# Four chunks and three parts of a product: part by part in place of chunk by chunk, with the weights at another place in their tiles

## The chip, the cores and the metric

The kernel runs on one core of a Trainium2 chip. Its engines each follow their own list of instructions and wait for each other through semaphores: TensorE (PE; its weight loads are shown apart as PEld), VectorE (DVE), ScalarE (ACT), GpSimd (POOL) and SyncE (SP), which issues most DMAs. The metric is the time of the device in microseconds for one whole execution, the median of several runs.

## The reference

One inference step of one decoder layer over 576 tokens: 512 of one new sequence and 8 x 8 of sampled sequences that have a retention state. Everything is float32.

```python
def swiglu(h, w_gate, w_up, w_down):
    return (jax.nn.silu(h @ w_gate) * (h @ w_up)) @ w_down
...
    h = modulate(rms_norm(x, n1_g), sh1, sc1)
    x = x + 0.5 * g1 * swiglu(h, w1_gate, w1_up, w1_down)
    h = modulate(rms_norm(x, nm_g), sh2, sc2)
    mix, S_new, v_rows = token_mix(h, pos0, S0, w_in, gm_ln_g, gm_ln_b, gm_ws, gm_bs, w_a, w_b, w_o)
    x = x + g2 * mix
    h = modulate(rms_norm(x, n2_g), sh3, sc3)
    x = x + 0.5 * g3 * swiglu(h, w2_gate, w2_up, w2_down)
```

The width is 1024, the inner width of each SwiGLU 2816. `token_mix` multiplies h by `w_in` (1024 x 10240), runs the gated spatial mixing and the retention over its columns, and goes back through `w_a`, `w_b` and `w_o`.

## The kernel before, in words

**Operands in two parts.** A float32 number is written as the sum of a high part, rounded to the format that a fast matmul takes (`F32R`), and a low part, the rest. ACT writes the high part by a copy; DVE then writes the low part, the source less the high part. A product of two such numbers takes three matmuls, high by high, high by low and low by high; low by low is dropped. In the code `wh, wl` are the parts of the weights, the left operand that is loaded into TensorE, and `xh, xl` those of the activations, the right operand that streams past.

**Pairs.** The gate and up columns of the two SwiGLUs, and most of `w_in`, go two columns of 128 at a time through seven block products of a Strassen-Winograd scheme in place of eight (class `Pair`; the first two pairs of each stage go plainly with eight, class `Plain`). The contraction of 1024 is split into two halves of 512, and the tokens into two halves of 288. So one block product, `prod` (line 647), is 512 x 128 by 512 x 288: four chunks of 128 of the contraction times three parts, twelve matmuls of 128 x 128 by 128 x 288 into one accumulator. There are 482 of them.

**Where the operands lie.** The right operands of `prod` are tiles `xa` and `xs` of 2 parts x 4 chunks x 288 elements: a chunk is 1152 bytes, the low part lies 4608 bytes behind the high one. They are made once for a stage, in two halves of two chunks (names such as `N11h0`, `N11h1`, `N11l0`, `N11l1` in the lists of steps: operand, part, half). The left operands are tiles `whl` (two column blocks) and, for `a12` alone, `whs` (one): 2 parts x blocks x 512 elements, with some elements of room. `put_hi` (line 664) takes a tile and lets ACT write the high part; `put_lo` lets DVE write the low part. `set_in` leaves the room partly ahead of the weights: they begin `at` elements into the tile. Every such tile begins at a multiple of 128 bytes. `whl` without an argument begins at `INTO`, 28 elements, which is 112 bytes. Other weights take `MID`, 45 elements or 180 bytes: those of the down projections (`wd`, `xw`, some `whl`) and of the mixing stage. One tile of `w_o`, `wo`, begins at 16 elements, 64 bytes. These go through `proj` (line 485), which has the same three matmuls for each chunk, with 320 or 256 tokens.

**What sets the order.** In the stages around a norm an order written out by hand (`BEGIN`, `INTO_MIX`, `INTO_FFN2`) says which step follows which, and each engine but SP is held to it. Elsewhere the calls of the code are placed by the scheduler of the programming layer, which at a few places puts matmuls of one product between those of another. A matmul waits for the last of its operands' writers, by a semaphore on the first matmul that needs it.

Of the kernel before, what the change touches and what calls it, by code (L numbers as in the profile page):

```python
# [15 lines left out]
P = 128  # L16
# [20 lines left out]

INTO = 28
MID = 45
HALF = (slice(0, H), slice(H, T))  # L40
PART = (slice(0, 320), slice(320, T))
PW = (320, T - 320)
# [42 lines left out]
def layer_kernel(ctx: ExitStack, tc: tile.TileContext, a):  # L85
# [7 lines left out]
    wp = ctx.enter_context(tc.tile_pool(name="wp", bufs=1))  # L93
# [16 lines left out]
    def nm(s):  # L110
        count[0] += 1
        return f"{s}_{count[0]}"


    now = {"wraw": None, "slu": None}
# [21 lines left out]
    def nine_w(shape):  # L137

        room = 9 * 256 - shape[1] * shape[2] * shape[3]
        return set_in(now["xs1"], shape, room, MID, tag="x", name=nm("xw"), bufs=3)  # L140

# [6 lines left out]
    def set_in(home, shape, room=INTO, at=INTO, **kw):  # L148

        n = 1  # L150
        for d in shape[1:]:
            n *= d
        t = home.tile([P, n + room], F32R, **kw)[:, at:at + n]
        if len(shape) == 4:
            return t.rearrange("p (a b c) -> p a b c", b=shape[2], c=shape[3])
        return t.rearrange("p (a b c d) -> p a b c d", b=shape[2], c=shape[3], d=shape[4])
# [9 lines left out]
    def whl(shape, at=INTO):  # L166
        small = len(shape) == 3 and shape[1] == 1
        tag = "whs" if small else "whl"
        return set_in(
            now["whs"] if small else wp, [P] + shape, INTO if small else 64, at,  # L170
            tag=tag, name=nm(tag), bufs=1 if small else 4,
        )

# [7 lines left out]
    def high_low(shape, at=INTO):  # L181
        t = whl([2] + shape, at)
        return t[:, 0], t[:, 1]
# [7 lines left out]
    def load_w(src, k0, kc, c0, cols, eng=None, at=INTO):  # L191
        return split_w(load_raw(src, k0, kc, c0, cols), eng, at)
# [39 lines left out]
    def tick(us):  # L232
        for s in list(side):
            s[1] -= us
            while s in side and s[1] <= 0:
                try:
                    s[1] += next(s[0])
                except StopIteration:
                    side.remove(s)
# [176 lines left out]
    class Norm:  # L416
# [4 lines left out]
        def square(self, x, h):  # L421
            if self.all is None:
                self.all = tp.tile([P, T], F32, tag="all", name=nm("all"), bufs=1)
                self.acc = [self.all[:, HALF[i]] for i in range(2)]
            first = self.n[h] == 0 and not self.t[h]
            t = self.acc[h] if first else half()
            self.t[h].append(t)
            ACT.activation(out=t, in_=x[:, HALF[h]], func=AF.Square)

# [65 lines left out]
    def cost(kc):  # L495
        return kc * 3 * 0.1225
# [26 lines left out]
    class Operands:  # L523
# [27 lines left out]
        def blocks(self, j):  # L551
            hb = self.hb
            return tuple(hb[:, c:c + 2, cl] for c in (2 * j, 4 + 2 * j) for cl in HALF)

# [56 lines left out]
    def norm_steps(st, n, O, h):  # L611
# [4 lines left out]
        for p in range(4):  # L616
            st[f"x{p}{h}"] = lambda p=p: O.x(p, n.r[h], HALF[h])
            for c in range(2):
                if h:
                    st[f"b{p}{c}"] = lambda p=p, c=c: O.b(2 * p + c, slice(H, NP))  # L620
                else:
                    st[f"b{p}{c}0"] = lambda p=p, c=c: O.b(2 * p + c, HALF[0])

# [22 lines left out]

    def prod(ps, w, x, fresh):
        (wh, wl), (xh, xl) = w, x
        for j in range(4):
            for z, (s, m) in enumerate(((wh, xh), (wh, xl), (wl, xh))):  # L650
                PE.matmul(  # L651
                    ps[:, :H], lhsT=s[:, j * P:(j + 1) * P], rhs=m[:, j, :],
                    start=fresh and j == 0 and z == 0, stop=j == 3 and z == 2, skip_group_check=True,
                )
        tick(cost(4))
# [6 lines left out]

    class Weights:
        def put_hi(self, names, src, neg=False):
            hl = whl([2, len(names), 512])
            if neg:
                ACT.activation(out=hl[:, 0], in_=src, func=AF.Copy, scale=-1.0)
            else:
                ACT.copy(out=hl[:, 0], in_=src)  # L669
            self.hl[names] = hl, src, neg  # L670
# [29 lines left out]
    class Plain(Weights):  # L700
# [22 lines left out]
        def h0a(self):  # L723
            self.A = [bank() for _ in range(2)]
            for ps, w in zip(self.A, ("n11", "n21")):
                prod(ps, self.w[w], op("N11"), True)
# [4 lines left out]
        def h1a(self):  # L731
            self.D = [bank() for _ in range(2)]
            for ps, w in zip(self.D, ("n11", "n21")):
                prod(ps, self.w[w], op("N1"), True)

        def h0b(self):
            for ps, w in zip(self.A, ("a12", "a22")):
                prod(ps, self.w[w], op("B21"), False)
# [5 lines left out]
        def e0s(self):  # L744
            self.g = self.g or self.gated()
            ACT.activation(out=self.g[:, HALF[0]], in_=self.A[0][:, :H], func=AF.Silu)

# [217 lines left out]
    def home_wd(c, shape):  # L965
        return set_in(now["hl"], shape, 64, MID, tag="wd", name=nm("wd"), bufs=2)

    def home_whl(c, shape):
        return home_wd(c, shape) if c in (0, 1, 4, 5) else whl(shape[1:], MID)

# [62 lines left out]
    for i in range(2):  # L1033
        for n in range(NT):
            m = P if n < 4 else NS
# [98 lines left out]
    def home1(c, shape):  # L1134
        if c in (6, 7):
            return nine_w(shape)
        return home_wd(c, shape) if c in (0, 1, 4, 5) else whl(shape[1:], MID)

# [400 lines left out]
    def weights_b(hds, j):  # L1539
        kc = 2 * len(hds)  # L1540
        return load_w(a["w_b"][0], 2 * hds[0], kc, j * (8 // kc) * P, 8 // kc * P, at=MID)

# [112 lines left out]
    def weights_u(g):  # L1655
        return load_w(win, 0, KC, U0 + g * P, P, at=MID)

# [78 lines left out]
    for i in range(2):  # L1736
        for n in range(NT):
            m, z = P if n < 4 else NS, NT * i + n
# [316 lines left out]
```

## Time and profile before

| | |
|---|---|
| median of 3 runs | 1657.79 us (1654.53 to 1658.67) |
| the profiled execution's own time | 1656.22 us |
| its span, first to last instruction | 1654.4 us |
| mean clock granted to TensorE | 0.996 |
| busy: PE, PEld, DVE, ACT, POOL | 1624.5, 1560.9, 1153.0, 784.3, 293.1 us |
| matmuls, weight loads | 12548, 12548 |
| of these in `prod`, line 651 | 5784 |
| moved by DMA | 252.09 MB, mean 152 GB/s |

A row of the profile names a line of the kernel (L651 is the matmul in `prod`, L485 that in `proj`, L669 and L679 the copies and subtractions of `put_hi` and `put_lo`, L564 and L571 those of the operands), an engine, an operation, and `out<-in` by the names of the tiles. Matmuls overlap: one of 288 columns takes some 294 ns from its start to its end, and the next begins long before that. How fast TensorE goes is read from the distance between starts, and in the rows in order of time from the start of one group to that of the next, divided by the count.

### The profile page before, as it was taken

The page shows a single profiled execution, that of the slowest core. Times are in us where ns is not written, and L with a number is a line of the kernel's source. Part 1 is how long each engine was busy: PE and PEld are TensorE (multiplying, and loading weights), DVE is VectorE, ACT ScalarE, POOL GpSimd, SP SyncE. Part 2 cuts the span into 40 slices and gives each one's busy share as a digit, 9 for nine tenths or more (in the row PEclk, how much of TensorE's full clock was granted, in tenths as well). Part 3 has the DMA queues.
Part 4 walks back from the last instruction along what each step waited for, and adds up shares of the span by engine and source line. Part 5 has one row for each costly group of instructions (what it writes and reads, how often), then busy time and mean ns, then how long its engine had stood idle before and what let it go on. Part 6 is the DMA issues. An engine that isn't in the chain of part 4 may idle for free. (4 is left out here: it accounts for less than half of the span.)

```text
span 1654.4 us, 31368 instructions
## 1 busy us (share of the span) xinstructions
PE 1624.5 (98%) x12548; PEld 1560.9 (94%) x12548; DVE 1153.0 (70%) x1835; ACT 784.3 (47%) x1331; POOL 293.1 (18%) x372
## 2 busy tenths in 40 slices
PE   8999999999999999999999999999999999999997
PEld 4899999999999999999999999998999999999997
DVE  6867857676697777854788554676848868676773
ACT  5634524344564556553444454453236525343454
POOL 0000000000411111113346343454231000000002
PEclk9999999999999999999999999999999999999999
DMA  9553444332536776765367575799540233332331
GB/s 301 145 156 109 141 133 136 114 103 87 179 117 209 227 213 189 222 192 192 121 192 251 180 171 159 207 262 271 172 141 14 87 93 96 95 92 81 99 89 58
DMA packets 300213, 252.09 MB, mean 152 GB/s; under 512 B 13594, under 2 KB 260634, under 8 KB 300067
## 3 DMA queue, kind: packets, MB, share of 16 engines
q1 hardware_dynamic: 284594, 206.76, 41.5%
q0 software_dynamic: 13168, 40.97, 8.9%
q10 hardware_dynamic: 2304, 2.36, 0.4%
q8 instruction: 98, 1.61, 0.4%
q14 instruction: 49, 0.39, 0.1%
HBM read 207.01 MB, written 43.02 MB: 151 GB/s over the span
## 5 line engine op out<-in xcount | busy, mean ns | idle before, releaser
L651 PE MATMUL ps<-xa,whl 128*128 128x288 f32 x3000 | 423.6, 296 | 5.8 <-ACT xa L564 2.4
L651 PEld LDWEIGHTS ps<-xa,whl 128*128 128x128 f32 x3000 | 404.5, 190 | 18.5 <-issue 4.2
L651 PE MATMUL ps<-xs,whl 128*128 128x288 f32 x2040 | 289.1, 295 | 0.9 <-ACT sn L660 0.5
L651 PEld LDWEIGHTS ps<-xs,whl 128*128 128x128 f32 x2040 | 274.0, 189 | 11.0 <-issue 4.2
L679 DVE TENSOR_TENSOR whl<-wraw,whl 128x1024 fp32r<-128x1024 f32 x192 | 234.4, 1223 | 55.0 <-ACT whl L669 46.7
L669 ACT CAST whl<-wraw 128x1024 fp32r<-128x1024 f32 x192 | 200.0, 1047 | 107.9 <-DVE wraw L793 65.9
L485 PEld LDWEIGHTS ps<-c,wd 128*128 128x128 f32 x1824 | 236.9, 188 | 3.5 <-issue 3.4
L485 PE MATMUL ps<-c,wd 128*128 128x320 f32 (+1 forms) x1824 | 240.0, 292 | 0.0
L485 PE MATMUL ps<-c,whl 128*128 128x256 f32 (+1 forms) x1368 | 186.9, 294 | 1.1 <-ACT c L195 0.7
L485 PEld LDWEIGHTS ps<-c,whl 128*128 128x128 f32 x1368 | 179.4, 188 | 3.4 <-ACT c L195 1.1
L472 POOL TENSOR_TENSOR x<-x,s 128x64 f32<-128x64 f32 x72 | 36.8, 511 | 797.4 <-DVE s L471 771.6
L466 DVE SCALAR_TENSOR_TENSOR x<-ps,gate,x 128x320 f32<-128x320 f32 (+1 forms) x128 | 61.1, 481 | 111.2 <-PE ps L485 111.1
L660 ACT COPY sn<-ps 128x288 f32<-128x288 f32 x195 | 77.4, 399 | 107.2 <-PE ps L651 106.9
L188 DVE TENSOR_TENSOR whl<-wraw,whl 128x1024 fp32r<-128x1024 f32 x56 | 76.3, 1364 | 66.2 <-ACT whl L187 65.4
L952 ACT CAST wd<-wraw 128x640 fp32r<-128x640 f32 (+2 forms) x58 | 45.4, 783 | 102.3 <-PE ps L485 93.4
L1353 PE MATMUL ps<-whl,xx 128*128 128x256 f32 x768 | 88.9, 276 | 0.0
L1353 PEld LDWEIGHTS ps<-whl,xx 128*128 128x128 f32 x768 | 88.0, 188 | 0.0
L651 PE MATMUL ps<-xs,whs 128*128 128x288 f32 x480 | 69.9, 294 | 0.0
L187 ACT CAST whl<-wraw 128x1024 fp32r<-128x1024 f32 x56 | 58.6, 1049 | 21.5 <-PE ps L485 13.3
L651 PEld LDWEIGHTS ps<-xs,whs 128*128 128x128 f32 x480 | 65.7, 189 | 0.0
L669 ACT CAST whs<-wraw 128x512 fp32r<-128x512 f32 x62 | 38.5, 620 | 56.5 <-PE ps L651 46.7
L957 DVE TENSOR_TENSOR wd<-wraw,wd 128x640 fp32r<-128x640 f32 (+2 forms) x58 | 53.5, 922 | 10.3 <-ACT wd L952 10.2
(285 smaller groups left out, 2220.6 us busy)
## 6 DMA issues: line engine op xcount, KB each, us to landing
ada<-in_w_ada_dram SPq DMA_DIRECT2D x56, 512.0 KB
wraw<-in_w_in_dram SPq DMA_DIRECT2D x96, 256.0 KB
wraw<-in_w_gate_dram SPq DMA_DIRECT2D x88, 256.0 KB
wraw<-in_w_up_dram SPq DMA_DIRECT2D x88, 256.0 KB
wraw<-in_w_in_dram SPq DMA_DIRECT2D x32, 512.0 KB
wraw<-in_w_down_dram SPq DMA_DIRECT2D x32, 384.0 KB
wraw<-in_w_down_dram SPq DMA_DIRECT2D x32, 320.0 KB
accd<-c POOLq DMA_DIRECT2D x32, 288.0 KB, 5.7
```

Source lines behind the costliest of these rows:

```text
L187: ACT.copy(out=hi, in_=raw)
L188: now["lo"] = (eng or DVE).tensor_tensor(out=lo, in0=raw, in1=hi.bitcast(F32), op=ALU.subtract)
L466: DVE.scalar_tensor_tensor(out=x[:, o:o + w], in0=ps[:, :w], scalar=g[:, c, 0:1], in1=x[:, o:o + w], op0=ALU.mult, op1=ALU.add)
L472: return lambda: POOL.tensor_tensor(out=x[:, NP:T], in0=x[:, NP:T], in1=u, op=ALU.add)
L485: PE.matmul(ps[:, :PW[h]], lhsT=s[:, k, c0:c0 + P], rhs=m[:, PART[h]], start=k == 0 and z == 0, stop=k == kc - 1 and z == 2,)
L651: PE.matmul(ps[:, :H], lhsT=s[:, j * P:(j + 1) * P], rhs=m[:, j, :], start=fresh and j == 0 and z == 0, stop=j == 3 and z == 2, skip_group ...
L660: ACT.copy(out=t, in_=ps[:, :H])
L669: ACT.copy(out=hl[:, 0], in_=src)
L679: now["lo"] = DVE.tensor_tensor(out=hl[:, 1], in0=src, in1=hl[:, 0].bitcast(F32), op=ALU.subtract)
L952: ACT.copy(out=hl[:, 0], in_=self.raw[c])
L957: DVE.tensor_tensor(out=lo, in0=self.raw[c], in1=hi.bitcast(F32), op=ALU.subtract)
L1353: PE.matmul(ps[:, :DV], lhsT=s, rhs=m, start=i == 0, stop=i == 23)
```

## The change

Three edits. `prod` has its loops swapped: the three parts are now the outer loop and the four chunks the inner one. The first part is high weights by the low operand, then high by high, then low weights by the high operand; before, high by high came first. And the weights that `put_hi` places begin 7 elements, 28 bytes, into their tile in place of 112; the small tiles have 64 elements of room in place of 28, and their weights begin at 39 elements, 156 bytes, which is again 28 past a multiple of 128. Other weights stay where they are, and so does the number of instructions.

```diff
@@ -37,6 +37,7 @@
 
 INTO = 28
 MID = 45
+EARLY = 7
 HALF = (slice(0, H), slice(H, T))
@@ -167,7 +168,7 @@
         small = len(shape) == 3 and shape[1] == 1
         tag = "whs" if small else "whl"
         return set_in(
-            now["whs"] if small else wp, [P] + shape, INTO if small else 64, at,
+            now["whs"] if small else wp, [P] + shape, 64, at + 32 if small else at,
             tag=tag, name=nm(tag), bufs=1 if small else 4,
         )
 
@@ -646,8 +647,8 @@
 
     def prod(ps, w, x, fresh):
         (wh, wl), (xh, xl) = w, x
-        for j in range(4):
-            for z, (s, m) in enumerate(((wh, xh), (wh, xl), (wl, xh))):
+        for z, (s, m) in enumerate(((wh, xl), (wh, xh), (wl, xh))):
+            for j in range(4):
                 PE.matmul(
                     ps[:, :H], lhsT=s[:, j * P:(j + 1) * P], rhs=m[:, j, :],
                     start=fresh and j == 0 and z == 0, stop=j == 3 and z == 2, skip_group_check=True,
@@ -662,7 +663,7 @@
 
     class Weights:
         def put_hi(self, names, src, neg=False):
-            hl = whl([2, len(names), 512])
+            hl = whl([2, len(names), 512], EARLY)
```

The order of the instructions is shown at three places. The first is on TensorE in the second SwiGLU's gate and up columns (1292.8 to 1294.5 us in the profile): a product with fresh weights `whl_14896`, whose high part comes from ACT and whose low part from DVE, and with it a second product from the other block of the same tile. Before:

```order
L651 MATMUL ps_14951<-xa_14584,whl_14896 128x288 [waits Activation_49]
L651 MATMUL ps_14951<-xa_14584,whl_14896 128x288
L651 MATMUL ps_14903<-xa_14693,whl_14896 128x288 x2
L651 MATMUL ps_14951<-xa_14584,whl_14896 128x288 [waits DVE_49]
L651 MATMUL ps_14951<-xa_14584,whl_14896 128x288 x9
L651 MATMUL ps_14903<-xa_14693,whl_14896 128x288 x10
```

With the change:

```order
L652 MATMUL ps_14951<-xa_14584,whl_14896 128x288 [waits Activation_49]
L652 MATMUL ps_14951<-xa_14584,whl_14896 128x288 x7
L652 MATMUL ps_14903<-xa_14693,whl_14896 128x288 x2
L652 MATMUL ps_14951<-xa_14584,whl_14896 128x288 [waits DVE_49]
L652 MATMUL ps_14951<-xa_14584,whl_14896 128x288 x3
L652 MATMUL ps_14903<-xa_14693,whl_14896 128x288 x10
```

Ten matmuls stand ahead of the wait for the low part in place of four. The same pair of products at 488.1 us has eleven there in place of four.

The second is on TensorE at the start of the mixing stage (445.5 us), the first product after the norm, whose right operand `xa_4965` comes half by half, its high parts from ACT and its low parts from DVE. Before:

```order
L651 MATMUL ps_4987<-xa_4965,whl_4763 128x288 [waits Activation_49]
L651 MATMUL ps_4987<-xa_4965,whl_4763 128x288 [waits DVE_49]
L651 MATMUL ps_4987<-xa_4965,whl_4763 128x288 x4
L651 MATMUL ps_4987<-xa_4965,whl_4763 128x288 [waits Activation_49]
L651 MATMUL ps_4987<-xa_4965,whl_4763 128x288 [waits DVE_49]
L651 MATMUL ps_4987<-xa_4965,whl_4763 128x288 x4
L651 MATMUL ps_4988<-xa_4965,whl_4763 128x288 x12
```

With the change:

```order
L652 MATMUL ps_4987<-xa_4965,whl_4763 128x288 [waits DVE_49]
L652 MATMUL ps_4987<-xa_4965,whl_4763 128x288
L652 MATMUL ps_4987<-xa_4965,whl_4763 128x288 [waits DVE_49]
L652 MATMUL ps_4987<-xa_4965,whl_4763 128x288
L652 MATMUL ps_4987<-xa_4965,whl_4763 128x288 [waits Activation_49]
L652 MATMUL ps_4987<-xa_4965,whl_4763 128x288
L652 MATMUL ps_4987<-xa_4965,whl_4763 128x288 [waits Activation_49]
L652 MATMUL ps_4987<-xa_4965,whl_4763 128x288 x5
```

The first matmul now waits for DVE's low part, and the third for the low part of the second half, which the eighth waited for.

The third is on TensorE in the first stage (53.7 us), where `xs_81_470`, the next right operand, is still being made. Before:

```order
L651 MATMUL ps_475<-xs_81_470,whl_423 128x288 x6
L651 MATMUL ps_475<-xs_81_470,whl_423 128x288 [waits Activation_49]
L651 MATMUL ps_475<-xs_81_470,whl_423 128x288 [waits DVE_49]
L651 MATMUL ps_475<-xs_81_470,whl_423 128x288 x4
L651 MATMUL ps_476<-xs_81_470,whl_423 128x288 x12
```

With the change:

```order
L652 MATMUL ps_475<-xs_81_470,whl_423 128x288 x2
L652 MATMUL ps_475<-xs_81_470,whl_423 128x288 [waits DVE_49]
L652 MATMUL ps_475<-xs_81_470,whl_423 128x288 x3
L652 MATMUL ps_475<-xs_81_470,whl_423 128x288 [waits Activation_49]
L652 MATMUL ps_475<-xs_81_470,whl_423 128x288 x5
```

DVE's second half is needed by the third matmul in place of the eighth.

## The prediction, made before the changed kernel was run

> **What bounds the kernel now.** I read the head of the page first, for who is busy, at what clock, and for how long.
>
> ```profile
> span 1654.4 us, 31368 instructions
> PE 1624.5 (98%) x12548; PEld 1560.9 (94%) x12548; DVE 1153.0 (70%) x1835; ACT 784.3 (47%) x1331; POOL 293.1 (18%) x372
> PEclk9999999999999999999999999999999999999999
> ```
>
> TensorE is busy for all but 30 us, at the full clock in every slice; the vector and scalar engines have slack. Since busy matmuls overlap, "98%" does not say that each one runs as fast as it can. So the questions are two: how long does TensorE stand still, and how far apart do its matmuls start while it runs.
>
> For the first I read who TensorE waited for. All its waits together are some 22 us, and the four rows of the line that the change touches are these (total, times, longest):
>
> ```profile
> PE ps L651 <- ACT xa L564: 2.4, 1, 2.4
> PE ps L651 <- ACT whl L669: 1.4, 1, 1.4
> PE ps L651 <- DVE whl L679: 1.3, 2, 0.8
> PE ps L651 <- DVE xa L571: 0.6, 1, 0.6
> ```
>
> Under 6 us: no reordering of waits can be worth much. For the second I read the view of that one line, L651, the matmul inside `prod` (duration: min/median/max in ns):
>
> ```profile
> L651 PE MATMUL ps<-xa,whl x3000: 289/293/607, 36.0 to 1602.9; 128*128 128x288 f32 x188
> L651 PE MATMUL ps<-xs,whl x2040: 289/293/515, 53.7 to 1598.9; 128*128 128x288 f32 x186
> L651 PE MATMUL ps<-xs,whs x480: 289/294/296, 67.9 to 1592.6; 128*128 128x288 f32 x160
> L651 PE MATMUL ps<-xa,whs x264: 289/294/402, 475.3 to 730.3; 128*128 128x288 f32 x132
> ```
>
> That is 3000 + 2040 + 480 + 264 = 5784 matmuls, all of one shape. The third row is the cleanest, since nothing interrupts it: equal work takes from 289 to 296 ns. Something other than the amount of work decides 7 ns of each matmul.
>
> The spacing is read from the rows in order of time: the start of a group taken from the start of the next, over the count.
>
> ```profile
> 1304.97 4.89 PE L651 MATMUL ps<-xa,whl 128*128 128x288 f32 x36
> 1309.70 1.74 PE L651 MATMUL ps<-xs,whl 128*128 128x288 f32 x12
> ...
> 421.66 5.32 PE L485 MATMUL ps<-c,wd 128*128 128x320 f32 x36
> 426.82 5.32 PE L485 MATMUL ps<-c,xw 128*128 128x320 f32 x36
> ...
> 434.02 2.20 PE L485 MATMUL ps<-c,wd 128*128 128x256 f32 x18
> 436.06 0.65 PE L444 MATMUL ps<-all,onesr 128*128 128x288 f32 x2
> ...
> 1235.69 3.68 PE L485 MATMUL ps<-xa,wo 128*128 128x320 f32 x24
> 1239.21 2.91 PE L485 MATMUL ps<-xa,xw 128*128 128x256 f32 x24
> ...
> 1248.11 2.99 PE L485 MATMUL ps<-xa,wo 128*128 128x256 f32 x24
> 1250.94 0.29 PE L651 MATMUL ps<-xs,whl 128*128 128x288 f32 x1
> ```
>
> In `prod`: 4.73 us over 36, 131.4 ns each. Its 288 columns lie halfway between the 256 and the 320 of L485, so L485 gives a yardstick. With `wd`, whose weights begin 45 elements, 180 bytes, into their tile (52 past a multiple of 128): 5.16/36 = 143.3 ns and 2.04/18 = 113.3 ns, halfway 128.3 ns. With `wo`, which begins 16 elements, 64 bytes, in: 3.52/24 = 146.7 and 2.83/24 = 117.9, halfway 132.3 ns. The same kind of matmul in the same loop thus costs 4 ns more or less with the tile that its weights are in, and the two tiles differ in where the weights begin. `prod`, beginning 112 bytes in, lies at 131.4, near the slower end.
>
> **The change part by part.** No instruction is added or removed: still 5784 matmuls with as many weight loads. Three things move.
>
> First, where the weights begin: 28 bytes past a multiple of 128 in place of 112. No row shows a start of 28. The bounds come from the nearest rows. Like `wd`, spacing falls by 131.4 - 128.3 = 3.1 ns, and 3.1 x 5784 = 17.9 us go. Like `wo`, it rises by 0.9 ns, 5.2 us. From `prod`'s own range: all matmuls at the least duration, 294 to 289, give 5 x 5784 = 29 us less; all at the most, 294 to 296, 12 us more. Of the three starts seen (52, 64, 112), 52 is nearest to 28, 24 bytes off against 36 and 44, but it lies on the far side, so I do not take its whole gain: two thirds, 2.1 ns, 12.1 us. It lies on the path that sets the end, since TensorE is that path; nothing covers it, and nothing else must speed up, for DVE is 30% idle.
>
> Second, the order inside `prod`. Before, the first two of each three matmuls shared a left operand, but each has a weight load of its own anyway (the counts of PE and PEld above are equal), so nothing is lost by parting them. The right operand used to be taken from the two parts of one chunk by turns, 4608 bytes apart, with a step of 1152 bytes to the next chunk every third time; now it walks chunk by chunk, 1152 bytes each time (odd multiples of 128 at the joins too). No row separates the two kinds of step, so its price is put at 0 within the bounds above and goes to a rival.
>
> Third, the waits. The low part of the weights is needed by the ninth matmul of a product in place of the third; the low part of the operand by the first in place of the second, and its chunks 2 and 3 by the third in place of the eighth. Four places show it (columns as before; in brackets the idle time and what ended it):
>
> ```profile
> 1292.82 0.79 PE L651 MATMUL ps<-xa,whl 128*128 128x288 f32 x4 [1.38 <-ACT whl L669]
> 1293.17 2.37 DVE L679 TENSOR_TENSOR whl<-wraw,whl 128x1024 fp32r<-128x1024 f32 x2
> 1294.44 1.33 PE L651 MATMUL ps<-xa,whl 128*128 128x288 f32 x4 [0.84 <-DVE whl L679]
> ...
> 488.12 0.79 PE L651 MATMUL ps<-xa,whl 128*128 128x288 f32 x4
> 489.42 1.75 PEld L651 LDWEIGHTS ps<-xa,whl 128*128 128x128 f32 x13 [0.73 <-DVE whl L679]
> 489.42 1.85 PE L651 MATMUL ps<-xa,whl 128*128 128x288 f32 x12 [0.50 <-DVE whl L679]
> ...
> 445.49 0.40 PE L651 MATMUL ps<-xa,whl 128*128 128x288 f32 x1 [2.41 <-ACT xa L564]
> 445.68 1.53 DVE L571 SCALAR_TENSOR_TENSOR xa<-x,xa 128x576 fp32r<-128x576 f32 x2
> 446.48 0.79 PE L651 MATMUL ps<-xa,whl 128*128 128x288 f32 x4 [0.59 <-DVE xa L571]
> ...
> 53.67 1.30 PE L651 MATMUL ps<-xs,whl 128*128 128x288 f32 x8
> 53.75 0.76 DVE L575 TENSOR_TENSOR xs<-hb,xs 128x576 fp32r<-128x576 f32 x1
> ```
>
> At 1292.82 and 488.12 the program now has ten and eleven matmuls ahead of the low part, 10 x 0.131 = 1.31 and 1.44 us of work against 1.62 and 1.30 us until it was there: of the 0.84 and 0.50 us waited, about 0.3 remains, so 1.0 us is won. At 445.49 the one matmul that ran before the low operand part has to wait for it too: its 0.13 us of work are lost, and the third matmul, due at 446.48 + 2 x 0.13 = 446.74, waits for the second half, ready at 445.68 + 1.53 = 447.21: 0.47 us more. At 53.67 the third matmul is due at 53.93 and its operand's second half comes at 54.51: 0.58 us lost, where before the eighth, due at 54.59, found it there. Sum: -1.0 + 0.13 + 0.47 + 0.58 = +0.2 us. Behind the waiting matmul stand only later matmuls; those who wait for them (the copies of ACT and the products of DVE) have more slack than that. If all three losses doubled, it would be 1.4 us.
>
> The writes to the weights keep their sizes; a start that is a multiple of four bytes stays one, so ACT and DVE are put at nothing, and their slack would cover a few per cent.
>
> The sum, against the profiled execution's own 1656.22 us (a span of 1654.4 and 1.8 around it; the median of the runs shown is 1657.79, 0.1% above): 1656.2 - 12.1 + 0.2 = 1644.3, so **1644 us**. About 0.3%, 5 us, is what a measurement of this kernel can tell from no change.
>
> **The rivals.** The first is slower: the walk of the right operand. In L485 the right operand's steps are even multiples of 128 bytes (2304, 18 of them); in `prod` four steps of every twelve are odd ones (1152, nine). If the odd steps alone carry the 3.1 ns by which `prod` exceeds the `wd` yardstick, each costs 3.1 x 3 = 9.3 ns; with twelve of twelve every matmul is 9.3 ns over 128.3, 6.2 above today: 36 us, 1692. The longest duration of the clean row, 296, speaks against so much; capped there, 2.3 ns over the median, it is 13 us: **1669 us**. For it speaks that L651 is the slow one of two lines that differ in just this; against it, that `wo`, with even steps alone, is slower still. It decides from a spacing of 132.3 ns on.
>
> The second is no change: the start and the walk do not matter, and `wd` and `wo` differ for another reason (they also lie elsewhere, beside other work). Then only the waits move: 1656.2 + 0.2 = **1656.4 us**. The Trainium skill, "TensorE: Matmul & The Clock Gate", Part 2 (step by step: what each phase is for), speaks for it: TensorE has two independent read ports, and the next weights' load takes nothing from the running matmul, so where the weights begin could not matter to it. The spread from 289 to 296 in one shape says that something does matter here.
>
> The third: 28 behaves as 64 does in `wo`, 0.9 ns more: 1656.2 + 5.2 + 0.2 = **1661.6 us**, on the edge of what can be told from no change.
>
> That the edit misses its aim can be excluded: every large and small weight tile of the pairs' products moves to the new start, and all 482 products to the new order.
>
> **How the numbers follow.** Forecast 0.55, with its own range from 1630 (4.5 ns less, near the floor of 289) to 1651 (0.9 ns less); the walk 0.22; no change 0.15; like `wo` 0.08. Faster by over 0.3%: 0.55. Within 0.3%: 0.15 and half of the third rival, 0.19. Slower: 0.22 and the other half, 0.26. The range leaves out the last of the gain below and the uncapped walk above: 1631 to 1669.
>
> **What would show it.** Right: the view of `prod`'s line has a median near 291 to 292, the 36 matmuls at 1304.97 take about 129.3 ns each, and the waits for the low weights shrink to 0.3 us. A median still at 293 to 294 with the time unchanged means that neither start nor walk matters. A median of 295 or more means the walk costs. If the time falls but the spacing of `prod` does not, the waits were mis-sized and the forecast is right by accident; a gain over 25 us would mean that the start takes away more than the spread seen here.

## The result, and the profile after

The changed kernel takes 1661.99 us, the median of six runs (1661.41 to 1664.28), against 1656.26 us for the kernel before in six runs (1654.53 to 1658.67). The ratio is 1.0039, with a 95% interval of 1.0028 to 1.0050: slower by some 6 us, where 12 us less had been forecast. Executions of one kernel differ by about as much with the clock granted: on one chip the kernel before spanned 1650.7 us at a mean clock of 0.998 and 1657.3 at 0.993.

The profiled execution of the changed kernel took 1664.28 us, at the upper end of its runs. The head of its page:

```profile
span 1662.5 us, 31375 instructions
PE 1632.4 (98%) x12548; PEld 1571.9 (95%) x12548; DVE 1153.2 (69%) x1835; ACT 784.4 (47%) x1331; POOL 293.2 (18%) x372
PEclk9999999999999999999999999999999999999999
```

The span is 8.1 us longer, TensorE is 7.9 us longer busy and its weight loads 11.0 us, no other engine by more than 0.2 us. The row of the clock has a 9 in every slice, as before, but a slice is some 41 us long and hides short spells. In the matmul of `prod`, before and then after (stretch, its length, TensorE busy, weight loads busy, granted clock, DMA):

```profile
447.80:451.20 3.40, 3.40 (x16) 3.13 (x14) 0.50 0.15 54
1294.30:1297.70 3.40, 3.26 (x13) 3.26 (x14) 0.50 0.57 167
```

```profile
448.40:455.20 6.80, 6.09 (x24) 5.80 (x24) 0.50 0.12 43
1301.70:1305.20 3.50, 3.50 (x17) 3.50 (x16) 0.51 0.62 180
```

In these spells half the clock was granted, for 6.8 us before and 10.3 after. Nearly all distances from one matmul's start to the next are exactly 240 ns there, 24 before and 33 after, which costs 2.6 and 3.5 us against the distances at full clock. So the spells explain about 1 us of the 8; for the rest TensorE took longer at full clock for the same matmuls. Which of them, the view of the matmul in `prod` shows (all lines below it stand one lower, so it is L652 now; duration in ns, min/median/max):

```profile
L652 PE MATMUL ps<-xa,whl x3000: 288/295/609, 36.0 to 1611.0; 128*128 128x288 f32 x188
L652 PE MATMUL ps<-xs,whl x2040: 288/295/507, 53.7 to 1607.0; 128*128 128x288 f32 x186
L652 PE MATMUL ps<-xs,whs x480: 288/293/299, 68.8 to 1600.6; 128*128 128x288 f32 x160
L652 PE MATMUL ps<-xa,whs x264: 292/295/403, 479.8 to 736.6; 128*128 128x288 f32 x132
```

The medians before were 293, 293, 294 and 294. The two large rows rose by 2 ns, the small tiles' rows stand at 293 and 295. The rows in order of time, at two places:

```profile
424.30 5.32 PE L486 MATMUL ps<-c,wd 128*128 128x320 f32 x36
429.46 5.32 PE L486 MATMUL ps<-c,xw 128*128 128x320 f32 x36
...
1311.40 4.96 PE L652 MATMUL ps<-xa,whl 128*128 128x288 f32 x36
1316.20 1.76 PE L652 MATMUL ps<-xs,whl 128*128 128x288 f32 x12
```

In `prod`, 4.80 us over 36 are 133.3 ns from start to start, where 131.4 stood before. The projections are untouched: 5.16/36 = 143.3 ns, to the digit what it was.

The same over the whole trace, from the start of each matmul to that of the next. A distance of over 160 ns has a wait in it, stands close behind one or lies in a spell of half clock (27 of the 94 before, 37 after); the rest is the running beat, at full clock. (Only neighbours of the same line count, 5734 in `prod`.)

| us | before | after |
|---|---|---|
| beat in `prod`, 5640 distances | 740.6 (131.32 ns each) | 751.2 (133.19 ns each) |
| the 94 distances over 160 ns in `prod` | 27.5 | 25.5 |
| projections | 520.3 | 520.3 |
| everything else between matmuls | 354.4 | 354.1 |

The whole difference is the beat: 1.87 ns on 5640 matmuls, +10.6 us, and 2.3 us less in waits and elsewhere (outside the spells, the distances over 160 ns fell from 67 with 20.0 us to 57 with 16.1). What TensorE waited for on this line (total, times, longest):

```profile
PE ps L652 <- DVE xa L572: 3.4, 1, 3.4
...
PE ps L652 <- ACT whl L670: 1.9, 1, 1.9
...
PE ps L652 <- DVE xs L576: 0.5, 1, 0.5
```

The two waits for the low weights (1.3 us) are gone, those for the operands have grown as the order makes them: the idle time of this line sums to 5.8 us, where it was 6.2.

So two questions were left for experiments: which of the two edits lengthens the beat, and why it does.

### The profile page after: what moved, and what is told of

The parts are those of the page before. It is cut to its first block, busy times and chain, and to the rows that moved or that the text cites. A ratio compares the mean times of both kernels' runs of the same rounds, so it can differ in the third digit from the quotient of the medians.

```text
span 1662.5 us, 31375 instructions
## 1 busy us (share of the span) xinstructions
PE 1632.4 (98%) x12548; PEld 1571.9 (95%) x12548; DVE 1153.2 (69%) x1835; ACT 784.4 (47%) x1331; POOL 293.2 (18%) x372
## 5 line engine op out<-in xcount | busy, mean ns | idle before, releaser
L652 PE MATMUL ps<-xa,whl 128*128 128x288 f32 x3000 | 429.3, 298 | 5.4 <-DVE xa L572 3.4
L652 PEld LDWEIGHTS ps<-xa,whl 128*128 128x128 f32 x3000 | 410.6, 189 | 17.5 <-DVE xa L572 3.9
L652 PE MATMUL ps<-xs,whl 128*128 128x288 f32 x2040 | 293.1, 296 | 0.5 <-DVE xs L576 0.5
L652 PEld LDWEIGHTS ps<-xs,whl 128*128 128x128 f32 x2040 | 277.9, 188 | 9.9 <-issue 5.0
L661 ACT COPY sn<-ps 128x288 f32<-128x288 f32 x195 | 77.6, 398 | 112.4 <-PE ps L652 111.5
L652 PE MATMUL ps<-xs,whs 128*128 128x288 f32 x480 | 70.4, 295 | 0.0
L652 PEld LDWEIGHTS ps<-xs,whs 128*128 128x128 f32 x480 | 66.1, 188 | 0.0
```

What stands on the lines that cost most here:

```text
L652: PE.matmul(ps[:, :H], lhsT=s[:, j * P:(j + 1) * P], rhs=m[:, j, :], start=fresh and j == 0 and z == 0, stop=j == 3 and z == 2, skip_group ...
L661: ACT.copy(out=t, in_=ps[:, :H])
```

## The experiments

Times are medians where a kernel was run several times; the others come from one run each, beside runs of the kernel before on the same chip (1655.7 to 1656.0 us in the first three groups). The beat is the mean distance as in the table above, from one profiled execution each.

### Each edit alone

The order alone: before, with only the loops of `prod` changed.

```diff
-        for j in range(4):
-            for z, (s, m) in enumerate(((wh, xh), (wh, xl), (wl, xh))):
+        for z, (s, m) in enumerate(((wh, xl), (wh, xh), (wl, xh))):
+            for j in range(4):
```

> Only the order inside a product is changed (part by part, low operand first); the weights begin at 112 bytes as before. Walk theory (each step of the right operand by an odd multiple of 128 bytes costs): the time is at least that of the whole change, 1662 us or more, and the matmuls of a product take a mean spacing of 133 ns or more; if steps and starts act together it may be as much as 135 ns, 1677 us. Start theory (28 bytes is a bad place, the order is neutral): 1656 us, 131.3 ns as before.

The start alone: the change, with the loops put back.

```diff
-        for z, (s, m) in enumerate(((wh, xl), (wh, xh), (wl, xh))):
-            for j in range(4):
+        for j in range(4):
+            for z, (s, m) in enumerate(((wh, xh), (wh, xl), (wl, xh))):
```

> Only the start of the weights is changed (28 past a multiple of 128 in place of 112); the order inside a product is chunk by chunk as before. Start theory: 1662 us, median duration of a product's matmul 295 ns. Walk theory: 1656 us or less, median 293 or 294 ns.

The order alone: 1658.82 us, ratio 1.0020 (1.0010 to 1.0031), beat 132.47 ns. The start alone: 1661.33 us, ratio 1.0029 (1.0016 to 1.0042), beat 132.34 ns. The rows of the order alone, then of the start alone, in order of time:

```profile
1309.26 4.93 PE L651 MATMUL ps<-xa,whl 128*128 128x288 f32 x36
1314.03 1.75 PE L651 MATMUL ps<-xs,whl 128*128 128x288 f32 x12
```

```profile
1310.19 4.92 PE L652 MATMUL ps<-xa,whl 128*128 128x288 f32 x36
1314.95 1.75 PE L652 MATMUL ps<-xs,whl 128*128 128x288 f32 x12
```

4.77/36 = 132.5 and 4.76/36 = 132.2 ns. Both edits lengthen the beat, by 1.15 and 1.02 ns over the whole line (6.5 and 5.8 us on 5640), and both together by 1.87: they do not quite add up. The waits for the low weights go with the order: the order alone has none any more, and the start alone has them as before (1.3 us in two). In time the start alone costs 5.6 us and the order alone 3.1. Two things on record make the latter less than its beat says: its waits shrank (outside the spells of half clock the distances over 160 ns cost 2.1 us less over the beat than before), and its profiled execution, with three spells of half clock, was among the two longest of its ten (1661.83 us).

### All starts, in either order

Is 28 bytes a bad start, or was 112 a good one? Two kernels let the start of each large weight tile go round sixteen places, one tile name for each; the small tiles keep theirs.

```diff
+    STARTS = (0, 4, 8, 12, 16, 20, 24, 28, 32, 36, 40, 44, 48, 52, 56, 60)
+    placed = [0]
+
+    def put_at(n):
+        if n == 1:
+            return whl([2, n, 512])
+        k = placed[0] % len(STARTS)
+        placed[0] += 1
+        return set_in(wp, [P, 2, n, 512], 64, STARTS[k], tag="whl", name=nm("at" + "abcdefghijklmnop"[k]), bufs=4)
...
-            hl = whl([2, len(names), 512])
+            hl = put_at(len(names))
```

> The order of before; the start of the large weight tiles goes round sixteen values, 0 to 240 bytes in steps of 16, tile after tile, and each tile is named by its start (ata 0, atb 16, ... ath 112, ... atp 240), so one trace has a mean duration for each. Start theory: the means differ by 3 ns or more from start to start, with ath (112) near 294 ns. Walk theory: all sixteen means are within 1 ns of each other. If what counts is the distance between weights and right operand within 256 bytes, starts 128 bytes apart give the same mean, since two of a product's four chunks lie on either side.

> The order of the change (part by part, low operand first); starts of 12 to 252 bytes in steps of 16, each tile named by its start (ata 12, atb 28, ... atp 252). Walk theory: every mean is at or above 294 ns, whatever the start. Start theory: the means spread by 3 ns or more, and atb (28) is among the slow ones; some start gives 291 ns or less.

They took 1661.19 and 1661.28 us. The beat by start, in ns, between matmuls of one tile (of a start and the one 128 bytes on; both, in this order, where they differ by over 0.2):

| order of before, bytes | 0 | 16 | 32 | 48 | 64 | 80 | 96 | 112 |
|---|---|---|---|---|---|---|---|---|
| beat | 133.1 | 133.0, 133.3 | 132.4 | 132.4, 132.2 | 132.4 | 133.6, 132.9 | 133.1, 133.8 | **131.5** |

| order of the change, bytes | 12 | 28 | 44 | 60 | 76 | 92 | 108 | 124 |
|---|---|---|---|---|---|---|---|---|
| beat | **131.8** | 133.0 | 132.3, 132.0 | 132.4, 131.9 | 133.6 | 133.0 | 131.8, 132.1 | 132.6 |

A start and its partner 128 bytes on agree within 0.4 ns in thirteen of the sixteen columns, so under either walk it is mostly the start modulo 128 that counts, and the differences are no accident of a place in the program. In the order of before, 112 is the fastest of the eight (28, which is not among them, had 132.3 ns in the start alone); in the order of the change, 28 is one of the slow ones and 12 the fastest. The mean over the eight starts is 132.7 ns in the order of before and 132.5 in that of the change. The same in rows: in the first kernel the tile at 112 bytes (the one at 144, with 133.3 ns, has a median of 296; its row stands further below), then in the second the tiles at 12, 28 and 204 bytes.

```profile
L651 PE MATMUL ps<-xs,ath x144: 289/294/400, 276.3 to 1551.1; 128*128 128x288 f32 x144
```

```profile
L651 PE MATMUL ps<-xa,ata x252: 288/294/607, 35.6 to 1599.1; 128*128 128x288 f32 x126
...
L651 PE MATMUL ps<-xa,atb x204: 291/295/306, 152.0 to 1591.0; 128*128 128x288 f32 x102
...
L651 PE MATMUL ps<-xa,atm x144: 291/297/303, 194.6 to 1572.0; 128*128 128x288 f32 x144
```

This settles what the change did. With its 131.3 ns the kernel before stood at the best start for its order, 1.4 ns below the mean; either edit leaves that place, and the change with its 133.2 lands 0.7 ns above the mean of its order.

Starts between those were tried later, at 4 and 8 modulo 16 bytes, in the same way.

> The order of before; the starts of the large weight tiles go round 4, 8, 20, 24, ... 116, 120 bytes, one tile name each (ata to atp). If the start of before (112) is one of the lucky ones and there is no much better: rows between 131.3 and 134 ns of spacing (durations 293 to 297), their mean near 132.5, the time near 1660 us. If 16-byte steps hid a fast start: one or two rows at 290 to 292.

> The order of the change; starts as in the other fine scan. If 12 bytes was the luckiest: rows between 131.5 and 134.5 ns of spacing (durations 293 to 297), the time near 1660 us. If there is a fast start: one or two rows at 290 to 292.

1663.30 and 1662.21 us. In the order of before the beat ran from 131.8 (100 bytes) to 135.4 (20 bytes), in that of the change from 132.0 (52) to 133.6 (20). No start is faster than the best seen before; the one at 20 is the slowest of all. In the first kernel its row, and the row of the start of 52 bytes from which the prediction took its gain:

```profile
L651 PE MATMUL ps<-xa,atc x240: 289/298/513, 43.5 to 1596.4; 128*128 128x288 f32 x120
...
L651 PE MATMUL ps<-xa,atg x156: 289/296/398, 170.4 to 1551.5; 128*128 128x288 f32 x156
```

At 52 bytes the beat of the products is 133.1 ns in the order of before and 132.0 in that of the change: both slower than the 131.3 of the kernel before.

### The change with another start

If the scan is right, one number mends most of the change.

```diff
-EARLY = 7
+EARLY = 3
```

> The change with one number altered: the weights begin 12 bytes into the row in place of 28 (and the small ones 140). In the scan of starts in the order of the change, the tile at 12 bytes had 131.8 ns a matmul and the one at 28 had 133.1: 1.3 x 5784 = 7.5 us less than the change: 1654.5 us (1651 to 1658), at or just below before. If a start's price in the scan was that of its place in the program, or of its neighbours in the round: as the change, 1662 us.

1657.20 us, ratio to before 1.0010 (0.9998 to 1.0021), beat 131.70 ns: 1.5 ns below the change, and what the scan had for this start (131.8). Moving the weights by 16 bytes takes back most of the loss: 1.4 us above the kernel before on the same chip, where the change was 5.7 above.

### The yardstick

The gain forecast came from the projections with `wd`: halfway between their 320 and 256 columns, 128.3 ns. Here they run at 288 columns themselves.

```diff
-PART = (slice(0, 320), slice(320, T))
-PW = (320, T - 320)
+PART = (slice(0, H), slice(H, T))
+PW = (H, T - H)
```

> Before with the projections' 576 columns divided 288 and 288 in place of 320 and 256; the products are untouched. If the yardstick of the prediction holds (halfway between 143.3 and 113.3 ns): 128.3 ns a matmul with wd at 288 columns, and the time stays, since 2 x 128.3 = 143.3 + 113.3. If halving was wrong, and 288 columns cost in the projections what they cost in the products: 131 to 133 ns; with 3 to 4 ns more on 4032 matmuls, 12 to 18 us slower: 1668 to 1674 us.

1666.63 us, 10.8 us more than before on the same chip, one run each. The rows in order of time:

```profile
425.17 4.90 PE L485 MATMUL ps<-c,wd 128*128 128x288 f32 x36
429.91 4.90 PE L485 MATMUL ps<-c,xw 128*128 128x288 f32 x36
...
437.05 2.56 PE L485 MATMUL ps<-c,wd 128*128 128x288 f32 x18
439.44 0.65 PE L444 MATMUL ps<-all,onesr 128*128 128x288 f32 x2
```

4.74/36 = 131.7 ns on the first half of the tokens and 2.39/18 = 132.8 on the second, not 128.3. Over the whole trace the projections take 534.3 us between their matmuls in place of 520.3: 3.5 ns more on each of 4032. (The time rose by less than these 14.0 us: in this execution there was no spell of half clock in `prod`.) So a matmul of the projections is no faster than one of the products when it is equally wide. The yardstick was the product of a straight line between two widths, and the line is not straight.

How the products' own matmuls depend on the width was asked of a kernel in which it goes round from product to product.

```diff
+        cols = 288 - 4 * (wide[0] % 16)
+        wide[0] += 1
...
-                    ps[:, :H], lhsT=s[:, j * P:(j + 1) * P], rhs=m[:, j, :],
+                    ps[:, :n], lhsT=s[:, j * P:(j + 1) * P], rhs=m[:, j, :n],
```

> Before, with the width of the products' matmuls going round from product to product: 288, 284, 280, ... 228 columns (the first matmul of a bank keeps 288, so that no column stays unwritten); the columns left out are not computed. Addresses, order and counts stay. If the time of a matmul is a straight line in its columns (as the prediction took it): 0.417 to 0.47 ns a column throughout, so 256 columns at 131.3 - 32 x 0.47 = 116.3 ns or, parallel to the clock, 118. If widths differ in what they lose (as 256, 288 and 320 do in the projections: 113.3, some 132, 143.3): the products at 256 come out near 113 to 114, and the spacing over the widths has steps.

The groups of one pair of tiles by width (busy us, mean ns of one):

```profile
L656 PE MATMUL ps<-xs,whs 128*128 128x284 f32 x33 | 4.8, 293 | 0.0
...
L656 PE MATMUL ps<-xs,whs 128*128 128x260 f32 x33 | 4.4, 281 | 0.0
...
L656 PE MATMUL ps<-xs,whs 128*128 128x244 f32 x33 | 4.2, 275 | 0.0
L656 PE MATMUL ps<-xs,whs 128*128 128x236 f32 x33 | 4.2, 274 | 0.0
L656 PE MATMUL ps<-xs,whs 128*128 128x232 f32 x33 | 4.2, 274 | 0.0
```

The beat is 132.5 ns at 288 columns, 125.3 at 272, 117.7 at 256, 113.2 at 244, and then stays: 112.3 at 240, 111.5 at 228. From 244 to 288 it is close to a straight line, 0.44 ns a column, with no step at 256. At 256 columns the products stand at 117.7 ns, where the projections with `wd` have 113.3 and those with `wo` 117.9. So it is the projections with `wd` that are fast at 256 columns (whether by their start was not tried); the products have no such width between 228 and 288. (The kernel as a whole took 1668.77 us: TensorE waited 50.6 us in `prod` for two writers, ACT's `sn` and DVE's `h`, where before had 0.5, and its mean clock over the span was 0.982. That the waits brought the lower clock was not tested.)

### Where the right operand and the weights lie to each other

In the trace of before, the second distance of each three (high weights by low operand, to low weights by high operand) is either 127 or 133 ns, by turns from chunk to chunk. The chunks of the right operand are 1152 bytes apart, an odd multiple of 128, while the weights of all chunks begin at one place modulo 256 bytes; so the two lie 112 bytes apart, modulo 256, at every other chunk, and 240 at the rest. From that came a theory: the distance of the two sets the beat. It was tested by moving the weights of the odd chunks 128 bytes further. The core of the edit, the rest being the views that follow from it:

```diff
+            ).rearrange("p (q x) -> p q x", q=2)[:, :, start:start + size]
+            hl = t.rearrange("p q (s y c) -> p q s y c", s=2, c=P)
+            src = src.rearrange("p m x -> p (m x)").rearrange("p (y q c) -> p q y c", q=2, c=P)
...
+                self.w[m] = tuple(
+                    [hl[:, (j + odd) % 2, s, 2 * i + j // 2, :] for j in range(4)] for s in range(2)
+                )
...
-        for j in range(4):
+        for j in (0, 2, 1, 3):
```

> Order of before (chunk by chunk, all three terms of a chunk together), but the chunks in the order 0, 2, 1, 3; and the weights of chunks 1 and 3 are put 128 bytes further, so that a weight block's place, modulo 256 bytes, stands always 112 bytes behind its chunk's. Theory (what counts is how far, modulo 256 bytes, the weights being loaded lie from the chunk being multiplied; single spacings in the trace of before are 127.1 ns where it is 112 and 133.2 ns where it is 240): 4820 of 5783 matmuls now have 112 and 963, at a change of chunk parity, have 240; mean about 128.1 ns against 131.3, so 3.2 x 5784 = 18.5 us less: 1637 us (1632 to 1643). Rival one (only the weights' own start modulo 128 counts, 112 as before): the spacing stays 131.3, 1656 us. Rival two (only odd steps of the right operand cost, two in twelve left in place of four): a gain here, and the same gain in the two runs beside it with this order.

> As the kernel with 112, same order of chunks, but with the two halves of the weights' tile exchanged, so that a weight block stands always 240 bytes from its chunk, modulo 256. Theory of the distance: 4816 of 5783 matmuls have 240, so about 133.2 ns, 1.9 x 5784 = 11 us more than before: 1667 us (1662 to 1672), and 25 us or more above the kernel with 112. Rival one (own start alone, 112 modulo 128 as before): 1656 us. Rival two (odd steps of the right operand alone): the same time as the kernel with 112.

> Before with one line changed: the chunks of a product in the order 0, 2, 1, 3. Nothing else moves; half of the matmuls have a distance of 112, half of 240. Theory of the distance: fewer changes, half at 127.1, half at 133.2, about 130.3 ns, 1.0 x 5784 = 6 us less: 1650 us (1646 to 1655). Rival one (start alone): 1656 us. Rival two (odd steps of the right operand alone): as the kernel with 112.

> The order of before, chunks 0, 1, 2, 3, with the weights of the odd chunks 128 bytes further as in the kernel with 112. Theory of the distance: 3854 of 5783 matmuls have 112, and 1929, one in three, at a change of chunk, have 240; 127.1 and about 133 give 129.1 ns, 2.2 x 5784 = 13 us less: 1643 us (1637 to 1650). Rival one (start alone): 1656 us. Rival two (odd steps alone, four in twelve as before): 1656 us.

| kernel | us | beat, ns | forecast by the distance |
|---|---|---|---|
| always 112, chunks 0, 2, 1, 3 | 1654.13, ratio 0.9983 (0.9973 to 0.9993) | 131.19 | 128.1 |
| always 240, chunks 0, 2, 1, 3 | 1653.74 (one run) | 131.48 | 133.2 |
| as before, chunks 0, 2, 1, 3 | 1657.87 (one run) | 131.76 | 130.3 |
| always 112, chunks 0, 1, 2, 3 | 1653.83 (one run) | 131.16 | 129.1 |

The theory fell: 112 and 240 differ by 0.3 ns, where 5.1 were forecast. How it fell is told by the distances one by one. The twelve of a product (the last leads to the next product), mean over all products with large weight tiles, in ns:

| | chunk 0 | chunk 1 | chunk 2 | chunk 3 |
|---|---|---|---|---|
| before | 131.8, 127.4, 131.2 | 131.1, 133.3, 133.2 | 131.7, 127.0, 130.9 | 130.9, 133.3, 133.5 |
| always 112, chunks 0, 1, 2, 3 | 132.9, 127.7, 133.8 | 132.2, 127.9, 133.4 | 132.6, 126.9, 134.3 | 132.4, 127.3, 132.9 |

The second distance came out at 127 in all four chunks, as it should; but most of those before and behind it rose, by 1 to 3 ns, and the mean stayed. A short distance is paid back by its neighbours. So one distance says nothing, only the mean over a product does. In the order 0, 2, 1, 3 not even the second distance obeyed: 131.6, 129.2, 129.6, 130.3 ns where it was always 112, and 129.6, 133.1, 129.0, 132.9 where it was always 240. The rows of the last kernel of the first table show the unchanged mean: medians of 293 on both tiles, as before.

```profile
L652 PE MATMUL ps<-xa,whl x3000: 288/293/609, 35.2 to 1600.6; 128*128 128x288 f32 x188
...
L652 PE MATMUL ps<-xs,whl x2040: 288/293/511, 52.9 to 1596.7; 128*128 128x288 f32 x186
```

The first kernel of that table is faster than the kernel before by 0.17%, with an interval that just leaves out no change, and so faster than the changed one too. It is not the gain forecast: of the 2.0 us by which its span is shorter, 0.7 are the beat, 0.7 the waits in `prod`, and the rest lies elsewhere.

### One operand held still

What has to move for the start to matter? Three kernels with the starts of the first scan, which compute something else than the reference: both operands of all twelve matmuls of a product the same, only the left one the same, only the right one.

```diff
-                    ps[:, :H], lhsT=s[:, j * P:(j + 1) * P], rhs=m[:, j, :],
+                    ps[:, :H], lhsT=wh[:, 0:P], rhs=xh[:, 0, :],
...
+                    ps[:, :H], lhsT=wh[:, 0:P], rhs=m[:, j, :],
...
+                    ps[:, :H], lhsT=s[:, j * P:(j + 1) * P], rhs=xh[:, 0, :],
```

> The products compute something else here: each of the twelve matmuls of a product multiplies the same weight block (chunk 0, high part) with the same operand chunk (chunk 0, high part); counts, sizes and weight loads stay. The start of the large weight tiles goes round 0 to 240 bytes in steps of 16, one tile name each (ata at 0, atb at 16, ... atp at 240). Nothing but the place of the weights against the operand now differs between tiles, and within a product nothing changes from matmul to matmul. If the place of one weight block against one operand chunk sets the spacing: the rows of the tiles spread by several ns, as single spacings of before do (127.1 to 133.2 ns; as durations, 162 more: 289 to 295). If it is the sequence (how the addresses change from one matmul to the next): all rows alike within 1 ns, and below 293 on the whole.

> Each of the twelve matmuls of a product takes the same weight block (chunk 0, high part); the right operand walks as before. Starts of the weight tiles as in the kernel with both operands fixed. If the walk of the right operand costs by itself (as the order alone suggested): the rows lie above those of the kernel with both fixed by about as much as the walk's part; 293 to 295. If it matters only together with the weights' walk: rows as with both fixed.

> Each of the twelve matmuls of a product takes the same operand chunk (chunk 0, high part); the weights walk as before. Starts of the weight tiles as in the kernel with both operands fixed. If a weight load's place against the running operand sets the spacing: all loads of a tile have one distance modulo 256, and the rows spread by the start over several ns, least near 112 bytes. If the right operand's walk is what costs: all rows alike, as with both fixed.

One tile, `atj`, which begins at 144 bytes: in the scan in the order of before, with the left operand held, with the right one held, and with both held.

```profile
L651 PE MATMUL ps<-xs,atj x180: 290/296/400, 85.0 to 1559.1; 128*128 128x288 f32 x180
L651 PE MATMUL ps<-xa,atj x132: 290/295/401, 181.6 to 1560.7; 128*128 128x288 f32 x132
```

```profile
L651 PE MATMUL ps<-xs,atj x180: 290/296/402, 85.4 to 1558.6; 128*128 128x288 f32 x180
L651 PE MATMUL ps<-xa,atj x132: 290/295/401, 183.3 to 1560.2; 128*128 128x288 f32 x132
```

```profile
L651 PE MATMUL ps<-xs,atj x180: 289/294/402, 84.8 to 1556.3; 128*128 128x288 f32 x180
L651 PE MATMUL ps<-xa,atj x132: 290/292/399, 181.8 to 1557.9; 128*128 128x288 f32 x132
```

```profile
L651 PE MATMUL ps<-xs,atj x180: 289/294/402, 86.3 to 1553.3; 128*128 128x288 f32 x180
L651 PE MATMUL ps<-xa,atj x132: 290/292/399, 183.0 to 1554.9; 128*128 128x288 f32 x132
```

In least and median duration the first two pairs of rows agree to the nanosecond, and so do the last two. It is so at all sixteen starts: beats with the left operand held agree with the scan within 0.1 ns, and with both held with those with only the right held, again within 0.1. So the walk of the weights from block to block costs nothing that these traces can show. The walk of the right operand does matter, but by no fixed price: holding it still makes the start of 144 bytes faster (133.3 to 131.2 ns) and that of 112 bytes slower (131.5 to 132.3). Over the whole line the mean is 132.2 ns held and 132.5 walking. And even where all twelve matmuls are the same, the beat depends on the start, from 131.1 to 133.4 ns; there a start and its partner 128 bytes on no longer agree (131.8 and 133.4 ns at 0 and 128), as they do where the right operand walks by odd multiples of 128.

The Trainium skill, "TensorE: Matmul & The Clock Gate", Part 2 (step by step: what each phase is for), which the prediction named for its second rival, has the two operands come through independent read ports. That rival took from this that the place of the weights could not matter. The runs of this case show otherwise: with everything else equal, the start of the weights alone moves the beat by up to 4 ns (131.5 ns at 112 bytes, 135.4 at 20). The spells of half clock bound what is open. There the distance is 240 ns in the kernel before, in the change and in each edit alone, so neither start nor order shows. Half of 240 is 120, and at full clock the beat lies 11 to 15 ns above that: it is this excess that start and order move. Where it comes from was not found.

## Why the prediction was wrong

It read rightly what bounds the kernel: TensorE's beat is the time, the waits are small, DVE and ACT have slack (their busy time did not move by more than 0.2 us). It asked the right question, the beat of `prod`, and answered it with the wrong sign. Its range, 1631 to 1669, held the time, through the rivals.

**The start, -12.1 us: the step that failed.** Measured alone, +1.02 ns a matmul, 5.8 us of beat, and 5.6 us in the time. Two things in it were wrong. The yardstick was not there: "halfway 128.3 ns" is 131.7 to 132.8 when it is run, and at the same 52 bytes the products take 133.1 (132.0 in the new order). And "28 is nearest to 52, so two thirds of its gain" took the starts for points on a smooth curve; in the scans neighbours four to sixteen bytes apart differ by up to 3 ns, either way. Without the yardstick the three starts seen said only that the beat varies by a few ns, and that before's was known and 28's was not.

**The order, 0 us: wrong too.** Measured alone, +1.15 ns, 6.5 us of beat, and 3.1 us in the time. It was left at zero because no row separated the two walks; what stood against zero, the walk rival, had a chance of 0.22.

**The waits, +0.2 us.** Of about the right size where they were forecast. Those were -1.0 at the low weights (measured -1.3), +0.60 at 445.5 us (+0.4: 3.38 against 2.41 + 0.59), and +0.58 at 53.7 us (+0.51); a half microsecond more came at a wait for high weights (1.4 to 1.9), and a half microsecond went at ACT's `sn`. What was not foreseen is that the distances over 160 ns would shrink by 2 us in all, although the spells of half clock grew. Part of it is a handful of distances of 0.3 to 0.6 us that fell or vanished; that a slower TensorE arrives later and so waits less is likely, but was not tested by itself.

**The projections and the other engines at nothing.** Right: 520.3 us between the projections' matmuls in both.

**The rivals.** The first, the walk of the right operand, had the direction, and the medians of 295 it named; but about half of the longer beat is the start's, which this sign could not tell apart. Its mechanism, a price on each odd step of 128 bytes, does not hold: with two odd steps in twelve in place of four (chunks 0, 2, 1, 3) the beat rose to 131.76, and with no step at all, at the same start, it was 132.3. The second, no change, is refuted by both edits alone. The third, 28 like 64, has by its 1661.6 the time that was measured, but not for its reason: it let the start alone cost 0.9 ns, which it does, and the order nothing, which is wrong. The sum of both, 1.9 ns or 10.6 us, is offset in part by the 2.3 us of waits, and the profiled execution lies another 2.3 us above the median of its kernel; that 1661.6 meets 1661.99 is luck.

**What better reading would have given.** Before has a beat of 131.3, and its rows range over 289 to 296. These are single durations, though, and the distances in it run from 127 to 133 ns by turns; a rate for the whole line cannot be taken from the shortest of them. Nothing in the profile says on which side an untried start and an untried order lie. The scans' answer, a mean of some 132.6 with most places between 131.5 and 133.6, is not in the trace of before; but a forecast near no change, with losses as likely as gains, was all that its rows could carry.

## What to carry to other kernels

A yardstick from other widths must be run at the width in question before a gain is taken from it: two widths on either side of 288 gave 128.3 ns, 288 itself 132. Where an equal matmul varies by a few ns with the places of its operands, an arbitrary move is a draw among those places; scan them, one tile name for each place, in one kernel, and take the best for the order that is used: 12 bytes against 28 was worth some 5 us. And judge a beat by its mean over a whole round, never by one distance in it, since neighbours pay back.

## What the runs showed of the hardware

- The beat of a 128x128 by 128x288 matmul of this kernel depends on where the weights begin, by up to 4 ns in 132 (131.5 at 112 bytes, 135.4 at 20), and which start is best depends on the walk of the right operand. Which weight block it loads next made no difference of over 0.1 ns, with all blocks at one place modulo 256 bytes.
- Twelve equal matmuls, with the same block and the same chunk, do not run at an even beat: with weights 80 bytes into their tile, distances from 126 to 137 ns stand side by side. Why is open, and so is why some places are faster on the mean.
- At half the granted clock the same matmuls start 240 ns apart, whatever the start and the order; at full clock they start 131 to 135 ns apart in place of half of that, 120.
- Below 244 columns a matmul with its own weight load is hardly shorter: 113.2 ns at 244, 111.5 at 228. Something other than the columns sets the beat there; what it is was not tried.
- In the projections 256 columns cost 113.3 ns with `wd` and 117.9 with `wo`, in the products 117.7; at 288 columns `wd` and the products both cost some 132. Splitting 576 tokens into 320 and 256 in place of 288 and 288 is worth 14 us over the projections of this kernel (520.3 against 534.3 us).
